# Layer norm and gate of a spatial-gating head group in pairs of 128-token tiles: one Gelu over 1024 columns for two tiles, PSUM emptied by a Copy, and a 2 KB GpSimd descriptor reserve

## The chip, the cores and the metric

The kernel runs on one NeuronCore of a Trainium2 chip. The metric is device time in microseconds (us) of one execution, lower is better. The time before the change is 2483.25 us, the median of three runs that lie between 2481.99 and 2483.38 us.

The core has five engines that run their own instruction streams in order and meet through semaphores: TensorE (PE, with its weight loads shown apart as PEld), VectorE (DVE), ScalarE (ACT), GpSimd (POOL) and SyncE (SP), which issues most DMA transfers. Matmul results land in PSUM banks; the other operands live in SBUF.

## The reference

One layer of an encoder over 2048 positions with 1024 channels. Only the first group of heads ("A", a gated MLP) is touched by the change; the second ("B", attention with a forget gate) runs beside it.

```python
h = rms_norm(x, norm_mix_g)
z = h @ w_in                                   # 1024 -> 2*512 + 3*512 + 8 columns
u_a = gelu(z[..., 0:512], approximate=False)
v_a = gelu(z[..., 512:1024], approximate=False)
# spatial gating, per block of 128 positions and per head of 64 channels
mu  = mean(v, axis=-1); var = mean((v - mu) ** 2, axis=-1)
vn  = (v - mu) * rsqrt(var + EPS) * ln_g
mixed = einsum('hts,bnshd->bnthd', masked w_s, vn) + b_s
out_a = u * mixed
# group B: softmax(q k^T / 8 + c[t] - c[s]) v, causal, c = cumsum(log sigmoid(f))
x = x + concat(out_a, out_b) @ w_out
x = x + conv_ffn(rms_norm(x)); out = rms_norm(x)
```

## The kernel before

All matrix products are in float32 split into a high and a low part, three matmuls for one (`mm3`, lines 202 to 212): line 207 (high by high), line 209 (high by low) and line 211 (low by high). Tokens are worked in two halves of 1024. Phase A of a half makes the projection `z`: keys and queries with channels on the partitions (`channels`, into `kx` and `qx`), values, and the two gated parts with tokens on the partitions (`token_major`). Phase B is attention; it has no stage of its own in the beginning but is fed as filler between the matmuls of phase A.

**The gated stage.** `gated` (line 467) is called at the end of half 0 and at the start of half 1, so the two calls follow each other. Each runs `token_major(512)`, the columns of `v`, and then `token_major(0)`, the columns of `u`: eight tiles of 128 tokens each, 24 matmuls (8 chunks by 3) of 512 columns per tile into one of two PSUM banks of the tag "mm". That makes 4 x 8 x 24 = 768 matmuls of this kind.

- For a tile of `v`, `a_layernorm` (line 520) applies Gelu straight from the PSUM bank into an SBUF tile "ln" (line 525, ACT) and then works by heads: sum (530, DVE), times 1/64 (531), subtract (532), square (535, ACT), sum (538, DVE), times 1/64 plus EPS (539), power of -0.5 (540, POOL), scale (543, DVE), times the gain (544, POOL). The result lies in one half of a pair tile "vn".
- For a tile of `u`, `a_mixed` (line 491) is called before every second tile and already works on pairs: the masked mixing matrix by the pair "vn" (498, PE) and the bias (500, DVE). `a_gate` (line 503) applies Gelu from PSUM (507, ACT), multiplies by "vn" (508, DVE) and, later, transposes the product on PE (`turn`, through line 182), splits it (188 on ACT, 189 on DVE) and stores both parts to DRAM (`mixh`, `mixl`, by SP).

**What sets the order.** `tick` counts the matmuls of `mm3`. `defer(n, fn)` runs `fn` in the program n matmuls later; `behind(n, fn)` does the same and also puts an order edge after the last matmul on the engine that the edge concerns. So the steps of the layer norm are spread at 5, 17, 25 and 40 matmuls after their tile, the gate's multiply at 5 and its transposes at 30 (`GATE_LAG`). The attention filler takes one step every 3.5 (half 0) or 4.0 (half 1) matmuls (`RATES`). A step of the filler is a score tile (lines 713 and 714 on PE, 717 or 719 on DVE for the row minimum, 722 on ACT for Exp with a sum), or a tile of the second pass (774 and 775 on PE, 778 on DVE, Exp at 780 on ACT, the split at 785 on ACT and 786 on DVE, and the product with the values at 762 and 763 on PE). Score tiles use three PSUM banks of the tag "s". From this the framework's planner makes one fixed order per engine, by priorities and by costs of its own.

Gelu and Exp (and Ln) need different function tables on ACT. The compiled program has an `ACT_TABLE_LOAD` wherever the table changes; the profile gives it the line of the instruction that needs it. Copy and Square have none in front of them.

Weights come as 128x1024 units: a DMA into "raw", a cast on POOL (149) and the rest on DVE (161).

The last argument of the program's constructor (line 1456) reserves a part of SBUF per partition for the descriptors of transfers that GpSimd issues. Those are 35 of the whole program, none of them in the gated stage: 22 at line 895, 11 at line 937 and 2 at line 1240.

Of the kernel before, what the change touches and what calls it, by code (L numbers as in the profile page):

```python
# [18 lines left out]
P = 128  # L19
# [6 lines left out]
TB = 512  # L26
# [9 lines left out]
GATE_LAG = 30  # L36
# [1 line left out]

BUFS = {
    "raw": 2, "rawl": 3, "whi": 5, "wlo": 5, "thi": 2, "tlo": 2, "acc": 4,  # L40
# [11 lines left out]
def f32(ap):  # L52
    return ap.bitcast(F32)
# [26 lines left out]
class Block:  # L80
# [323 lines left out]
    def a_half(self, half):  # L404
        nc, sp, pp = self.nc, self.sp, self.ap
# [17 lines left out]
        def token_major(col):  # L423
            us = [self.load_unit(self.w_in[:, 2 * j:2 * j + 2, col:col + 512], 512) for j in range(4)]
            wh = [us[k // 2][0][:, k % 2, :] for k in range(KC)]
            wl = [us[k // 2][1][:, k % 2, :] for k in range(KC)]
            for t in range(8):
                ps = self.til(pp, [P, TB], F32, "mm")
                tsl = slice((t % 4) * P, (t % 4 + 1) * P)
                self.mm3(ps, part(t // 4, 0, tsl), part(t // 4, 1, tsl), wh, wl)  # L430
                yield t, ps
# [35 lines left out]
        def gated():  # L467
            vns = []
            for t, ps in token_major(512):
                if t % 2 == 0:  # L470
                    vns.append(self.til(sp, [P, 2, TB], F32, "vn"))
                self.a_layernorm(ps, vns[-1][:, t % 2, :])
            for t, ps in token_major(0):
                if t % 2 == 0:
                    self.a_mixed(vns[t // 2])
                self.a_gate(half * 2 + t // 4, t % 4, ps, vns[t // 2][:, t % 2, :])
                if half == 0 and t % 4 == 3:
                    self.a_norm(1, t // 4, self.scales[t // 4], 14 if t == 3 else 16, 9 if t == 3 else 6)

        if half == 0:  # L480
            keys_queries()
            values()
            self.start_fill(self.b_stream([(h, tb) for tb in range(4) for h in range(8)]), RATES[0])
            gated()
        else:
            self.rate = RATES[1]
            gated()
            values()
            keys_queries()
# [10 lines left out]
                nc.vector.tensor_tensor(v[:, :, t, :], pg[:, :, t, :],  # L500
                                        self.sgb[:, 4 * q:4 * q + 4].unsqueeze(2).broadcast_to([P, 4, 64]), op=ALU.add)

    def a_gate(self, blk, t, pu, vn):

        nc, sp, pp = self.nc, self.sp, self.ap
        u = self.til(sp, [P, TB], F32, "u")
        nc.scalar.activation(u, pu, AF.Gelu)  # L507
        self.behind(5, lambda: nc.vector.tensor_tensor(u, u, vn, op=ALU.mult))

        def turn():  # L510
            hi = self.til(sp, [P, TB], F32R, "st")
            lo = self.til(sp, [P, TB], F32R, "st")
            self.transpose_split(pp, "tp", [u[:, c * P:(c + 1) * P] for c in range(4)], None, hi, lo)
            for r, dst in ((hi, self.mixh[blk]), (lo, self.mixl[blk])):
                self.dma(dst[0:512, t * P:(t + 1) * P].rearrange("(c p) t -> p c t", p=P),
                         f32(r).rearrange("p (c t) -> p c t", c=4))

        self.defer(GATE_LAG, turn)

    def a_layernorm(self, ps, vn):  # L520
        nc, sp = self.nc, self.sp
        h3 = lambda t: t.rearrange("p (h d) -> p h d", h=8)
        bc = lambda t: t.unsqueeze(2).broadcast_to([P, 8, 64])
        v = self.til(sp, [P, TB], F32, "ln")
        nc.scalar.activation(v, ps, AF.Gelu)  # L525
        mu, s2, r = [self.til(sp, [P, 8], F32, "lns") for _ in range(3)]


        def mean():
            nc.vector.tensor_reduce(mu, h3(v), axis=AX.X, op=ALU.add)  # L530
            nc.vector.tensor_scalar(mu, mu, 1.0 / 64, None, ALU.mult)
            nc.vector.tensor_tensor(h3(v), h3(v), bc(mu), op=ALU.subtract)

        def squares():
            nc.scalar.activation(vn, v, AF.Square)

        def variance():
            nc.vector.tensor_reduce(s2, h3(vn), axis=AX.X, op=ALU.add)
            nc.vector.tensor_scalar(s2, s2, 1.0 / 64, EPS, ALU.mult, ALU.add)
            nc.gpsimd.tensor_tensor(r, s2, self.mhalf, op=ALU.pow)  # L540

        def scale():
            nc.vector.tensor_tensor(h3(v), h3(v), bc(r), op=ALU.mult)
            nc.gpsimd.tensor_tensor(vn, v, self.lng, op=ALU.mult)

        for n, fn in ((5, mean), (17, squares), (25, variance), (40, scale)):
            self.behind(n, fn)

    def a_forget(self, half, b):
# [917 lines left out]
```

## Time and profile before

| What | Value |
|---|---|
| Runs | 2481.99, 2483.38, 2483.25 us; median 2483.25 us |
| Profiled execution | 2483.0 us |
| Its span, first to last instruction | 2481.3 us, so 1.7 us lie around it |
| Granted TensorE clock over the span | 0.995 |
| Busy share of the span | PE 98%, PEld 80%, DVE 70%, ACT 55%, POOL 14% |
| Gated stage (both halves) | about 186 to 466 us from the start of the span |

How to read it: a busy share is a mean over stages with different limits. Durations of matmuls are modelled and overlap, so a busy PE is not PE at its best pace; the distance from one matmul's start to the next shows the pace. "Idle before" is the time an engine stood still ahead of an instruction, and the arrow names what ended it. Line numbers are those of the kernel before.

### The profile page before, as it was taken

What the parts mean: (1) busy time and instruction counts of PE and PEld (TensorE: products, weight loads), DVE (VectorE), ACT (ScalarE), POOL (GpSimd) and SP (SyncE); (2) the same over time, 40 slices, a digit from 0 to 9 for tenths busy, and PEclk for the clock granted to TensorE, in tenths of its full rate; (3) what the DMA queues carried; (4) which work ended last, traced back from release to release, by engine and by line L of the source; (5) the groups of instructions that cost most, each with busy time, mean ns of one, the idle gap of its engine ahead of it and who ended that gap; (6) DMA issues with size and microseconds to landing.
All of it is one profiled execution on the core that took longest, in us unless ns stands there. A gap on an engine that the chain in (4) does not pass through costs nothing.

```text
span 2481.3 us, 33045 instructions
## 1 busy us (share of the span) xinstructions
PE 2430.5 (98%) x11082; PEld 1995.2 (80%) x11082; DVE 1742.9 (70%) x3116; ACT 1367.4 (55%) x2651; POOL 335.6 (14%) x343
## 2 busy tenths in 40 slices
PE   7998999999999999999999999999999999999998
PEld 5786878878788888888888888878888887888887
DVE  6237677655456878878787775488888887957776
ACT  4327778554355556766677673265555555444443
POOL 3214233010014111211111110100000000001000
PEclk9999999999999999999999999999999999999999
DMA  6863544766867545555555455412222228538633
GB/s 205 239 155 89 155 144 127 189 157 186 284 186 244 156 149 169 176 169 163 175 161 159 154 176 202 144 60 86 92 77 77 93 78 310 169 98 286 210 117 122
DMA packets 346246, 396.35 MB, mean 160 GB/s; under 512 B 52924, under 2 KB 222084, under 8 KB 344652
## 3 DMA queue, kind: packets, MB, share of 16 engines
q1 hardware_dynamic: 341036, 370.11, 48.8%
q0 software_dynamic: 5040, 24.12, 2.5%
q8 instruction: 88, 1.44, 0.2%
q14 instruction: 82, 0.67, 0.1%
HBM read 300.56 MB, written 93.72 MB: 159 GB/s over the span
## 4 chain that ended last, share of the span: by engine, by line
PE 81%; DVE 3%; ACT 2%; DMA 2%; issue 1%; POOL 1%; SPq 0%; DVEq 0%; POOLq 0%; ACTq 0%
PE D L1323 16%; PE mm L209 11%; PE mm L207 11%; PE mm L211 11%; PE A L1120 3%; PE A L1122 3%; PE A L1121 3%; PE o L763 2%; PE o L762 2%; PE s L714 2%; PE s L774 2%; PE s L775 2%; PE s L713 2%; PE B L1121 2%; PE B L1122 2%; PE B L1120 2%
## 5 line engine op out<-in xcount | busy, mean ns | idle before, releaser
L207 PE MATMUL mm<-thi,whi 128*128 128x512 f32 x960 | 378.4, 394 | 0.7 <-DVE vn L417 0.7
L209 PE MATMUL mm<-tlo,whi 128*128 128x512 f32 x960 | 377.5, 393 | 0.0
L211 PE MATMUL mm<-thi,wlo 128*128 128x512 f32 x960 | 377.1, 393 | 0.2 <-DVE wlo L161 0.2
L207 PE MATMUL mm<-whi,thi 128*128 128x512 f32 x640 | 254.4, 399 | 1.8 <-ACT ln L525 1.0
L209 PE MATMUL mm<-wlo,thi 128*128 128x512 f32 x640 | 253.5, 396 | 0.3 <-DVE wlo L161 0.2
L149 POOL TENSOR_SCALAR whi<-raw 128x1024 fp32r<-128x1024 f32 x108 | 127.0, 1176 | 935.6 <-PE mm L209 581.5
L211 PE MATMUL mm<-whi,tlo 128*128 128x512 f32 x640 | 253.3, 396 | 0.0
L722 ACT ACTIVATE s<-s,part 128x512 f32<-128x512 f32 (+3 forms) x257 | 150.7, 587 | 116.7 <-DVE part L717 60.3
L207 PEld LDWEIGHTS mm<-thi,whi 128*128 128x128 f32 x960 | 180.9, 188 | 39.1 <-DVE vn L417 1.1
L211 PEld LDWEIGHTS mm<-thi,wlo 128*128 128x128 f32 x960 | 180.9, 188 | 37.9 <-DVE wlo L161 0.7
L209 PEld LDWEIGHTS mm<-tlo,whi 128*128 128x128 f32 x960 | 180.9, 188 | 37.6
L786 DVE TENSOR_TENSOR pl<-e,ph 128x512 fp32r<-128x512 f32 (+2 forms) x212 | 131.7, 629 | 63.4 <-PE o L763 34.6
L161 DVE TENSOR_TENSOR wlo<-raw,whi 128x1024 fp32r<-128x1024 f32 x108 | 138.2, 1280 | 51.2 <-POOL whi L149 49.7
L780 ACT ACTIVATE e<-s 128x512 f32<-128x512 f32 (+2 forms) x227 | 116.5, 528 | 80.3 <-DVE s L778 38.3
L785 ACT ACTIVATE ph<-e 128x512 fp32r<-128x512 f32 (+2 forms) x212 | 117.4, 562 | 47.5 <-PE o L762 36.7
L207 PEld LDWEIGHTS mm<-whi,thi 128*128 128x128 f32 x640 | 121.7, 190 | 26.5 <-ACT u L507 1.6
L1323 PE MATMUL D<-wl,xh 128*128 128x512 f32 x368 | 141.3, 389 | 0.0
L209 PEld LDWEIGHTS mm<-wlo,thi 128*128 128x128 f32 x640 | 121.7, 190 | 24.3 <-DVE wlo L161 1.0
L1323 PE MATMUL D<-wh,xh 128*128 128x512 f32 x368 | 140.8, 389 | 0.2 <-DVE xo L1401 0.2
L211 PEld LDWEIGHTS mm<-whi,tlo 128*128 128x128 f32 x640 | 121.7, 190 | 24.0
L1323 PE MATMUL D<-wh,xl 128*128 128x512 f32 x368 | 137.2, 389 | 0.0
L717 DVE TENSOR_REDUCE part<-s 128x1 f32<-128x512 f32 x144 | 94.9, 683 | 29.0 <-PE s L714 28.9
(1883 smaller groups left out, 5837.6 us busy)
## 6 DMA issues: line engine op xcount, KB each, us to landing
raw<-in_w_up_dram SPq DMA_DIRECT2D x72, 512.0 KB
m<-kx SPq DMA_DIRECT2D x133, 256.0 KB
m<-kx SPq DMA_DIRECT2D x160, 136.0 KB
x<-act SPq DMA_DIRECT2D x84, 256.0 KB
raw<-in_w_in_dram SPq DMA_DIRECT2D x40, 512.0 KB
v<-vd SPq DMA_DIRECT2D x66, 256.0 KB
x<-in_x_dram SPq DMA_DIRECT2D x24, 512.0 KB
raw<-in_w_out_dram SPq DMA_DIRECT2D x24, 512.0 KB
```

What stands on the lines that cost most here:

```text
L149: self.cast_ins = self.nc.gpsimd.tensor_scalar(out, in_, 1.0, 0.0, ALU.mult, ALU.add).ins
L161: nc.vector.tensor_tensor(lo, raw, f32(hi), op=ALU.subtract)
L207: mm(ps, lhsT=ah[k], rhs=bh[k], start=k == 0, stop=False)
L209: mm(ps, lhsT=ah[k], rhs=bl[k], start=False, stop=False)
L211: self.last_mm = mm(ps, lhsT=al[k], rhs=bh[k], start=False, stop=k == n - 1).ins
L722: nc.scalar.activation(ps[:, :n], ps[:, :n], AF.Exp, scale=-1.0, bias=dst, accum_out=ls[:, tt, sb:sb + 1])
L785: nc.scalar.activation(ph[:, c], e[:, c], AF.Copy)
L786: nc.vector.tensor_tensor(pl[:, c], e[:, c], f32(ph[:, c]), op=ALU.subtract)
L1120: mm(ps, lhsT=xh[:, ks], rhs=yh[:, k, :], start=fresh and k == 0, stop=False, **kw)
L1121: mm(ps, lhsT=xh[:, ks], rhs=yl[:, k, :], start=False, stop=False, **kw)
L1122: mm(ps, lhsT=xl[:, ks], rhs=yh[:, k, :], start=False, stop=k == 3, **kw)
L1323: nc.tensor.matmul(bank[t], lhsT=x[i][:, ts], rhs=w[k], start=fresh and j == 0 and i + k == 0, stop=last and i == 1, **kw)
```

## The change

The layer norm and the gate take two tiles of 128 tokens at a time. Each PSUM bank is emptied by a Copy on ACT into one half of a pair tile of 1024 columns ("ln" for `v`, "u" for `u`). After the second tile, one Gelu over 1024 columns runs in place in SBUF, 3 matmuls later, and the following steps work on 1024 columns with 16 heads: sum, subtract, square, power, scale and the gate's multiply. The gain's multiply on POOL stays in two pieces of 512. The steps stand at 3, 9, 20, 28 and 44 matmuls after the pair's last matmul, the gate's multiply at 9 and the two tiles' transposes at 30 and 38. The pair tiles are twice as large; "ln" has 2 buffers for 3, "u" keeps 2, and the reserve for GpSimd's descriptors goes from 8192 to 2048 bytes per partition.

```diff
-    "x": 4, "st": 4, "ln": 3, "vn": 4, "u": 2, "lns": 9, "fs": 9, "fr": 3,
+    "x": 4, "st": 4, "ln": 2, "vn": 4, "u": 2, "lns": 9, "fs": 9, "fr": 3,
@@ gated
             for t, ps in token_major(512):
                 if t % 2 == 0:
+                    v = self.til(sp, [P, 2, TB], F32, "ln")
+                nc.scalar.activation(v[:, t % 2, :], ps, AF.Copy)
+                if t % 2:
                     vns.append(self.til(sp, [P, 2, TB], F32, "vn"))
-                self.a_layernorm(ps, vns[-1][:, t % 2, :])
+                    self.a_layernorm(v, vns[-1])
             for t, ps in token_major(0):
                 if t % 2 == 0:
                     self.a_mixed(vns[t // 2])
-                self.a_gate(half * 2 + t // 4, t % 4, ps, vns[t // 2][:, t % 2, :])
+                    u = self.til(sp, [P, 2, TB], F32, "u")
+                nc.scalar.activation(u[:, t % 2, :], ps, AF.Copy)
+                if t % 2:
+                    self.a_gate(half * 2 + t // 4, t % 4, u, vns[t // 2])
@@ a_gate
-        u = self.til(sp, [P, TB], F32, "u")
-        nc.scalar.activation(u, pu, AF.Gelu)
-        self.behind(5, lambda: nc.vector.tensor_tensor(u, u, vn, op=ALU.mult))
+        self.behind(3, lambda: nc.scalar.activation(u, u, AF.Gelu))
+        self.behind(9, lambda: nc.vector.tensor_tensor(u, u, vn, op=ALU.mult))
...
-        self.defer(GATE_LAG, turn)
+        self.defer(GATE_LAG, lambda: turn(0))
+        self.defer(GATE_LAG + 8, lambda: turn(1))
@@ a_layernorm
-        v = self.til(sp, [P, TB], F32, "ln")
-        nc.scalar.activation(v, ps, AF.Gelu)
-        mu, s2, r = [self.til(sp, [P, 8], F32, "lns") for _ in range(3)]
+        mu, s2, r = [self.til(sp, [P, 16], F32, "lns") for _ in range(3)]
+        half16 = self.mhalf[:, 0:1].broadcast_to([P, 16])
+        def gelu():
+            nc.scalar.activation(v, v, AF.Gelu)
...
-            nc.gpsimd.tensor_tensor(r, s2, self.mhalf, op=ALU.pow)
+            nc.gpsimd.tensor_tensor(r, s2, half16, op=ALU.pow)
 
         def scale():
             nc.vector.tensor_tensor(h3(v), h3(v), bc(r), op=ALU.mult)
-            nc.gpsimd.tensor_tensor(vn, v, self.lng, op=ALU.mult)
+            for j in range(2):
+                nc.gpsimd.tensor_tensor(vn[:, j, :], v[:, j, :], self.lng, op=ALU.mult)
 
-        for n, fn in ((5, mean), (17, squares), (25, variance), (40, scale)):
+        for n, fn in ((3, gelu), (9, mean), (20, squares), (28, variance), (44, scale)):
             self.behind(n, fn)
@@ kernel
-    nc = _bacc.Bacc("TRN2", target_bir_lowering=False, num_devices=1, dynamic_dma_scratch_size=8192)
+    nc = _bacc.Bacc("TRN2", target_bir_lowering=False, num_devices=1, dynamic_dma_scratch_size=2048)
```

More of the change, by code (lines that the diff above doesn't have):

```diff
@@ L501, in a_mixed, with a_gate, turn, a_layernorm @@
                                         self.sgb[:, 4 * q:4 * q + 4].unsqueeze(2).broadcast_to([P, 4, 64]), op=ALU.add)
-    def a_gate(self, blk, t, pu, vn):
+    def a_gate(self, blk, t, u, vn):
         nc, sp, pp = self.nc, self.sp, self.ap
-        u = self.til(sp, [P, TB], F32, "u")
-        nc.scalar.activation(u, pu, AF.Gelu)
-        self.behind(5, lambda: nc.vector.tensor_tensor(u, u, vn, op=ALU.mult))
-        def turn():
+        self.behind(3, lambda: nc.scalar.activation(u, u, AF.Gelu))
+        self.behind(9, lambda: nc.vector.tensor_tensor(u, u, vn, op=ALU.mult))
+        def turn(j):
             hi = self.til(sp, [P, TB], F32R, "st")
             lo = self.til(sp, [P, TB], F32R, "st")
-            self.transpose_split(pp, "tp", [u[:, c * P:(c + 1) * P] for c in range(4)], None, hi, lo)
+            self.transpose_split(pp, "tp", [u[:, j, c * P:(c + 1) * P] for c in range(4)], None, hi, lo)
+            tj = t - 1 + j
             for r, dst in ((hi, self.mixh[blk]), (lo, self.mixl[blk])):
-                self.dma(dst[0:512, t * P:(t + 1) * P].rearrange("(c p) t -> p c t", p=P),
+                self.dma(dst[0:512, tj * P:(tj + 1) * P].rearrange("(c p) t -> p c t", p=P),
                          f32(r).rearrange("p (c t) -> p c t", c=4))
-        self.defer(GATE_LAG, turn)
-    def a_layernorm(self, ps, vn):
+        self.defer(GATE_LAG, lambda: turn(0))
+        self.defer(GATE_LAG + 8, lambda: turn(1))
+    def a_layernorm(self, v, vn):
         nc, sp = self.nc, self.sp
-        h3 = lambda t: t.rearrange("p (h d) -> p h d", h=8)
-        bc = lambda t: t.unsqueeze(2).broadcast_to([P, 8, 64])
-        v = self.til(sp, [P, TB], F32, "ln")
-        nc.scalar.activation(v, ps, AF.Gelu)
-        mu, s2, r = [self.til(sp, [P, 8], F32, "lns") for _ in range(3)]
+        h3 = lambda t: t.rearrange("p t (h d) -> p (t h) d", h=8)
+        bc = lambda t: t.unsqueeze(2).broadcast_to([P, 16, 64])
+        mu, s2, r = [self.til(sp, [P, 16], F32, "lns") for _ in range(3)]
+        half16 = self.mhalf[:, 0:1].broadcast_to([P, 16])
+        def gelu():
+            nc.scalar.activation(v, v, AF.Gelu)
         def mean():
```

## The prediction

> **What bounds the kernel now.** I read the page first, then the busy times by stretch, the waits of PE, the instruction groups of ACT inside the gated stage, and last the timeline round one wait. The page says that PE sets the time:
>
> ```profile
> span 2481.3 us, 33045 instructions
> PE 2430.5 (98%) x11082; PEld 1995.2 (80%) x11082; DVE 1742.9 (70%) x3116; ACT 1367.4 (55%) x2651; POOL 335.6 (14%) x343
> ```
>
> The change leaves PE's matmuls as they are, so it can only win back time in which PE stands still or runs slowly. Busy times by stretch (length, then PE, PEld, DVE, ACT, POOL, granted clock, DMA share, GB/s), for the gated stage and for the stage behind it:
>
> ```profile
> 186.00:466.00 280.00, 267.04 (x1329) 219.39 (x1328) 199.73 (x446) 208.53 (x366) 82.07 (x65) 0.98 0.46 134
> 466.00:600.00 134.00, 134.00 (x628) 106.77 (x627) 75.05 (x173) 68.26 (x153) 9.78 (x8) 1.00 0.66 176
> ```
>
> PE idles 280.00 - 267.04 = 13.0 us in the gated stage and nothing in the 134 us behind it, where the same filler runs without Gelu. ACT is at 208.53 / 280 = 74% in the first and 51% in the second. The waits of PE in the gated stage (total us, times, longest):
>
> ```profile
> PE s L774 <- ACT s L722: 7.3, 6, 2.3
> PE o L762 <- ACT ph L785: 1.4, 2, 1.0
> PE s L774 <- ACT e L780: 1.3, 2, 1.0
> PE mm L207 <- ACT ln L525: 1.0, 1, 1.0
> PE mm L207 <- ACT u L507: 0.9, 2, 0.6
> ```
>
> These five add to 11.9 us of the 13.0, and all wait for ACT; the remaining rows name DVE, none a DMA. The groups of ACT in the stage (busy us, mean ns | idle before):
>
> ```profile
> L722 ACT ACT_TABLE_LOAD x17 | 21.8, 1283 | 5.4 <-DVE part L719 3.1 <-DVE part L717 2.0
> L507 ACT ACT_TABLE_LOAD x16 | 20.5, 1283 | 0.3
> L525 ACT ACT_TABLE_LOAD x15 | 19.2, 1283 | 0.3
> L780 ACT ACT_TABLE_LOAD x13 | 16.7, 1283 | 0.2
> L535 ACT ACTIVATE vn<-ln 128x512 f32<-128x512 f32 x16 | 10.1, 633 | 20.7 <-DVE ln L532 13.5 <-issue 7.2
> L507 ACT ACTIVATE u<-mm 128x512 f32<-128x512 f32 x16 | 9.6, 599 | 0.2
> L525 ACT ACTIVATE ln<-mm 128x512 f32<-128x512 f32 x16 | 9.5, 599 | 0.2
> L188 ACT ACTIVATE st<-tp 128x512 fp32r<-128x512 f32 x15 | 8.9, 594 | 0.7 <-PE tp L182 0.7
> ```
>
> Nearly every Gelu pays a table load (15 + 16 for 32), and the filler's next Exp pays one back (17 + 13): 61 loads, 78.2 us. How that becomes a PE wait, in the timeline (start, us, engine, line; idle before and its releaser in brackets), ACT, DVE and PE in turn, and then three stretches of 20 us with ACT's busy time and the granted clock:
>
> ```profile
> 347.66 1.28 ACT L525 ACT_TABLE_LOAD   x1
> 348.95 0.60 ACT L525 ACTIVATE ln<-mm 128x512 f32<-128x512 f32 x1
> 351.07 1.28 ACT L722 ACT_TABLE_LOAD   x1 [1.53 <-DVE part L719]
> ```
>
> ```profile
> 349.58 0.69 DVE L530 TENSOR_REDUCE lns<-ln 128x8 f32<-128x512 f32 x1 [1.07 <-ACT ln L525]
> 350.30 0.17 DVE L531 TENSOR_SCALAR lns<-lns 128x8 f32<-128x8 f32 x1
> 350.38 0.56 DVE L719 CUSTOM_DVE_ANT_0 s<-s,mask 128x384 f32<-128x384 f32 x1
> ```
>
> ```profile
> 350.62 0.39 PE L209 MATMUL mm<-wlo,thi 128*128 128x512 f32 x1
> 350.85 0.39 PE L211 MATMUL mm<-whi,tlo 128*128 128x512 f32 x1
> 353.10 0.47 PE L774 MATMUL s<-t,m 128*128 128x384 f32 x1 [1.86 <-ACT s L722]
> 353.38 0.51 PE L775 MATMUL s<-t,m 128*128 128x384 f32 x1
> 353.68 0.63 PE L207 MATMUL mm<-whi,thi 128*128 128x512 f32 x1
> ...
> 356.67 0.45 PE L209 MATMUL mm<-wlo,thi 128*128 128x512 f32 x1
> ```
>
> ```profile
> 206.00:226.00 20.00, 12.83 (x22) 0.91 0.18 59
> 246.00:266.00 20.00, 13.60 (x23) 0.91 0.49 144
> 346.00:366.00 20.00, 16.86 (x32) 0.91 0.30 85
> ```
>
> Gelu comes late because of its load, the layer norm's sum on DVE waits for it, the filler's row minimum (719) is queued behind that sum, ACT loads the Exp table only then, and PE, out of score banks, waits 1.86 us. After that the clock is down: the seven matmuls from 353.68 to 356.67 take 2.99 us instead of 7 x 0.23 = 1.61, so 1.4 us more. Three stretches show such a drop, 4.2 us together. **What is at stake is 11.9 + 4.2 = 16.1 us.**
>
> [...]
>
> **The change part by part.** *ACT.* Rows for operations of 1024 columns, and what they replace on DVE:
>
> ```profile
> L1237 ACT ACTIVATE cv<-ts 128x1024 f32<-128x1024 f32 x22 | 23.3, 1060 | 16.0 <-DVE ts L1233 16.0
> L1239 DVE TENSOR_TENSOR ts<-ts 128x1024 f32<-128x1024 f32 x22 | 26.8, 1220 | 0.0
> L530 DVE TENSOR_REDUCE lns<-ln 128x8 f32<-128x512 f32 x16 | 10.9, 684 | 14.7 <-ACT ln L525 14.6
> ```
>
> Removed: 78.2 of loads, 9.6 + 9.5 of Gelu, 10.1 of squares, 107.4 us. Added: 32 Copies out of PSUM at 0.594 (L188, which never has a load ahead) are 19.0; 16 Gelus at 1.06 are 17.0; 8 squares at 1.06 are 8.5; 16 loads for Gelu and at most 16 back are 32 x 1.283 = 41.1. That is 85.6 us, so ACT does 21.8 us less and falls from 74% to 67% of the stage.
>
> [...]
>
> *Banks.* The two rows of L207 that wait for Gelu (1.0 + 0.9) go: a Copy frees the bank after 0.6 us with no load ahead. What covers the Copy is the second "mm" bank, filled in 24 matmuls; without that cover it would cost 32 x 0.6 = 19 us.
>
> *Visits of Gelu.* The other ACT waits and the clock, 10.0 + 4.2 = 14.2 us, hang on ACT changing tables: 31 visits become 16, so half of it, 7.1 us, goes. Each visit that is left holds ACT 1.06 - 0.60 = 0.46 us longer and DVE 1.22 - 0.68 = 0.54 us longer at a piece, up to 1.0 us together. This price is not in the trace. Below, it is nothing: most visits cause no wait today. Above, every one of the 16 pays 1.0, 16 us. Only three waits today come with the clock drop, that is, are at the limit; half of that with some margin is one visit, so I take 1.0 us.
>
> *DVE.* Two operations of 512 (2 x 0.684) become one of 1.22, 0.15 less; with five such per pair and 8 pairs, 40 x 0.15 = 6 us less work. I count it at nothing, since DVE is 71% busy and its order matters more than its sum.
>
> *POOL and the reserve.*
>
> ```profile
> L540 POOL TENSOR_TENSOR lns<-lns,mhalf 128x8 f32<-128x8 f32 x16 | 27.8, 1736 | 66.1 <-DVE lns L539 56.7 <-DVE m L730 4.8 <-DVE mx L728 3.2
> L544 POOL TENSOR_TENSOR vn<-ln,lng 128x512 f32<-128x512 f32 x16 | 24.1, 1507 | 19.8 <-DVE ln L543 11.0 <-ACT ph L195 3.2 <-DVE lns L531 3.2
> L176 POOL TENSOR_TENSOR rstd<-rs,mhalf 128x1 f32<-128x1 f32 x16 | 9.5, 593 | 1.3
> act<-va POOLq DMA_DIRECT2D x22, 512.0 KB, 4.5
> ```
>
> The power of 16 columns lies between 1.74 and 2 x 1.74 = 3.47 us; on the line through 1 and 8 columns, 0.593 and 1.736, it is 1.736 + 8 x 0.163 = 3.04. Behind it on DVE waits the scale step, and behind that the filler. A matmul's slot in the stage is 280 / 768 = 0.365 us, so the scale stands 16 x 0.365 = 5.8 us after the variance, which needs 1.22 + 0.17 (L531's like) + 3.04 = 4.4: covered with 1.4 us to spare, where there were 15 x 0.365 - (0.68 + 0.17 + 1.74) = 2.9 before. If that cover were gone, 8 pairs at up to 1.4 us each would lose 11 us. The pair tile "ln" must be free 72 matmuls after its last one; scale (44), 1.22 and two products of 1.51 leave over 5 us. The stores of two tiles come 8 matmuls apart rather than 24; SP's filler loads behind them are covered, since no PE wait of the stage names a DMA. The smaller reserve costs nothing unless a transfer must wait for the one before: 4.5 us to land against a spacing of a whole pair of up-projection units, with POOL 14% busy. If that cover were gone, each of the 35 would hold POOL for about 4 us.
>
> **Sum.** 1.9 + 7.1 - 1.0 = 8.0 us out of the profiled execution's 2483.0 (1.7 more than its span): **2475.0 us**. The median of the runs, 2483.25, is the same to 0.01%. Behind the stage nothing takes the gain back that I can see: PE has no idle time from 466 to 600 us.
>
> **The rivals.**
>
> 1. *The waits only move* (no change by measure). For it: the 1.86 us wait hung on the order DVE has, sum before row minimum, and that order stays with a longer sum; the mean stands 6 matmuls, 2.2 us, behind a Gelu that needs 1.28 + 1.06 = 2.34. Against it: half as many such places. Then only the 1.9 us of the banks are sure: about 2481.
> 2. *The longer hold breaks the filler* (slower). Place: the three score banks at L774. A visit now keeps Exp off ACT for 1.28 + 1.06 + 1.28 = 3.6 us, before 3.2. If that is past what three banks cover, each visit makes a wait like the longest, 2.3 us, with 1.4 of slow clock: 3.7. Today's stake is met from 16.1 / 3.7 = 4.4 visits on; with 6 to 8 of 16 it is 22 to 30 us against 16.1, so 2489 to 2497. For it: waits of 2.3 already exist at 3.2. Against it: most of 31 visits cause none.
> 3. *It clears the stage.* All idle time and slow clock go, 13.0 + 4.2: 2483.0 - 17.2 = 2466. For it: the stage behind, with ACT at 51%, has none. Against it: ACT stays at 67%.
> 4. *Loads do not fall to 32*, since the planner may put Exp between the Copies and the Gelu without a saving: not likely, as Copy needs no table and the Gelus are 16 in number.
>
> **How the numbers follow.** About 0.2%, 5 us, is what a measurement of this kernel can tell from no change. Forecast (gain of 5 to 12 us) 0.43; rival 3 0.12; rival 1 0.25; rival 2 0.19; rival 4 0.01, at no change. So faster 0.55, same 0.26, slower 0.19. The likeliest one's own range is 2471 to 2478. The range to hold 8 in 10 takes the stake and a little for a new order of the planner's below, 2464, and rival 2's first half above, 2491.
>
> **What would show it.** In the stage: about 32 table loads with Gelu's rows 16; no PE wait at L207 for ACT; ACT near 187 us; PE's idle time near 6 us and one or two stretches below full clock instead of three. Wrong would be: PE idle at 13 us or more with half the loads; a wait at the Copy for "ln"; the scale step waiting for POOL in every pair; or a difference that lies behind 466 us.

## The result and the profile after

The changed kernel takes 2470.30 us (median of 5 runs, 2464.07 to 2473.17); the kernel before took 2481.99 us in the same series (5 runs, 2480.32 to 2483.38). The ratio is 0.995, with a 95% interval from 0.9935 to 0.9965. The profiled execution took 2470.3 us against 2483.0. So the change is faster by 11.7 us, 0.5%; the forecast was 8.0 us faster, 2475.0, in a range of 2464 to 2491.

Line numbers after the change are higher than before: 713 is now 724, 717 is 728, 719 is 730, 722 is 733, 762 is 773, 763 is 774, 774 is 785, 780 is 791, 785 is 796 and 786 is 797. The two Copies are 472 and 480, the two Gelus 537 and 512, the power 550, the scale 553 and the gain 555.

The head of the page after, and the busy times by stretch (columns as in the prediction):

```profile
span 2468.5 us, 32938 instructions
PE 2423.2 (98%) x11082; PEld 1992.3 (81%) x11082; DVE 1738.5 (70%) x3060; ACT 1341.4 (54%) x2629; POOL 329.2 (13%) x335
```

```profile
0.00:186.00 186.00, 171.00 (x793) 135.79 (x794) 76.80 (x152) 63.68 (x118) 44.81 (x69) 1.00 0.72 205
186.00:466.00 280.00, 273.00 (x1390) 228.68 (x1389) 203.31 (x405) 191.97 (x358) 77.48 (x56) 0.99 0.49 143
466.00:600.00 134.00, 134.00 (x627) 107.25 (x626) 73.57 (x166) 64.66 (x147) 9.06 (x8) 1.00 0.65 174
```

PE does the same 11082 matmuls. In the gated stage its idle time is 280.00 - 273.00 = 7.0 us, before 13.0, and ACT is busy for 191.97 us, before 208.53. PE ran 1390 matmuls in the same 280 us, before 1329: the stage itself became shorter. The waits of PE in it (total us, times, longest):

```profile
PE o L774 <- DVE pl L797: 2.1, 2, 1.7
PE s L758 <- DVE m L742: 1.9, 1, 1.9
PE s L724 <- DMA t<-qx: 1.9, 1, 1.9
PE s L785 <- ACT s L733: 0.5, 1, 0.5
```

The first row of before, 7.3 us for Exp (then L774 for L722), is down to 0.5 us, and nothing waits at L207 for Gelu any more. What is left waits for DVE and for one transfer. The groups of ACT in the stage, the table loads and the new operations (busy us, mean ns | idle before):

```profile
L733 ACT ACT_TABLE_LOAD x10 | 12.8, 1283 | 0.2
L537 ACT ACT_TABLE_LOAD x8 | 10.3, 1283 | 0.1
L512 ACT ACT_TABLE_LOAD x8 | 10.3, 1283 | 0.1
L480 ACT ACTIVATE u<-mm 128x512 f32<-128x512 f32 x16 | 9.6, 599 | 8.3 <-PE mm L211 8.2
L472 ACT ACTIVATE ln<-mm 128x512 f32<-128x512 f32 x15 | 8.7, 595 | 3.5 <-PE mm L211 3.4
...
L512 ACT ACTIVATE u<-u 128x1024 f32<-128x1024 f32 x8 | 8.5, 1061 | 0.1
L537 ACT ACTIVATE ln<-ln 128x1024 f32<-128x1024 f32 x8 | 8.5, 1060 | 0.1
L791 ACT ACT_TABLE_LOAD x5 | 6.4, 1283 | 0.1
```

Loads: 10 + 8 + 8 + 5 = 31 in place of 61, 39.8 us in place of 78.2. Each kernel has one load more in this window, for a small Exp of the filler (L748, before L737), so all in all there are 32 for 62. Both Gelu rows have 8 instructions and 8 loads, one load per visit.

**Where the time came from.** The windows above do not hold the same work in the two kernels, so I also counted along the work itself. Between the starts of two matmuls of the projection, I subtracted from the time that passed the length of every matmul in between at full pace (0.227 us for 512 columns, 0.175 for 384, 0.119 for 256, 0.108 for 128, read off the timelines). What is left is time that PE lost to waits and to a slow clock. The full-pace work is 2391.4 us in both kernels; the loss went from 73.5 to 60.7 us:

| Part (by projection matmuls) | lost before, us | lost after, us | difference |
|---|---|---|---|
| ahead of the gated stage (first 24 tiles) | 16.8 | 12.5 | -4.3 |
| gated stage (tiles 24 to 56) | 27.1 | 13.8 | -13.3 |
| behind it | 29.6 | 34.4 | +4.8 |

Two of the three rows are not what the prediction was about. The first row turned out to have a cause of its own. The last is worth little: counted in the same way, `before_no_gelu` (below), which has the order of the kernel before, loses 33.7 us there and not 29.6, and over the 14 profiles of this case that row lies between 27.8 and 36.2.

### The profile page after: what moved, and what is told of

The parts are those of the page before. It is cut to its first block, busy times and chain, and to the rows that moved or that the text cites. A ratio compares the mean times of both kernels' runs of the same rounds, so it can differ in the third digit from the quotient of the medians.

```text
span 2468.5 us, 32938 instructions
## 1 busy us (share of the span) xinstructions
PE 2423.2 (98%) x11082; PEld 1992.3 (81%) x11082; DVE 1738.5 (70%) x3060; ACT 1341.4 (54%) x2629; POOL 329.2 (13%) x335
## 4 chain that ended last, share of the span: by engine, by line
PE 83%; DMA 6%; DVE 5%; issue 2%; ACT 2%; POOL 1%; SPq 0%; POOLq 0%; DVEq 0%; ACTq 0%
PE D L1334 14%; PE mm L211 12%; PE mm L207 12%; PE mm L209 12%; PE A L1131 3%; PE A L1133 3%; PE A L1132 3%; PE o L774 2%; PE o L773 2%; PE s L786 2%; PE s L785 2%; PE B L1133 2%; PE B L1132 2%; PE B L1131 2%; PE s L724 2%
## 5 line engine op out<-in xcount | busy, mean ns | idle before, releaser
L207 PE MATMUL mm<-thi,whi 128*128 128x512 f32 x960 | 377.8, 394 | 1.7 <-DVE vn L417 1.4
L207 PE MATMUL mm<-whi,thi 128*128 128x512 f32 x640 | 253.7, 397 | 3.2 <-DVE acc L860 3.1
L207 PEld LDWEIGHTS mm<-thi,whi 128*128 128x128 f32 x960 | 180.5, 188 | 40.6 <-DVE vn L417 2.0
L797 DVE TENSOR_TENSOR pl<-e,ph 128x512 fp32r<-128x512 f32 (+2 forms) x212 | 136.6, 651 | 74.0 <-PE o L774 41.0
L207 PEld LDWEIGHTS mm<-whi,thi 128*128 128x128 f32 x640 | 121.0, 189 | 27.5 <-DVE acc L860 3.5
L209 PEld LDWEIGHTS mm<-wlo,thi 128*128 128x128 f32 x640 | 121.0, 189 | 23.3 <-DVE wlo L161 0.4
```

The lines of the kernel that those rows point to most:

```text
L207: mm(ps, lhsT=ah[k], rhs=bh[k], start=k == 0, stop=False)
L209: mm(ps, lhsT=ah[k], rhs=bl[k], start=False, stop=False)
L797: nc.vector.tensor_tensor(pl[:, c], e[:, c], f32(ph[:, c]), op=ALU.subtract)
```

## The experiments

Nearly every edit of this kernel makes the planner lay out all engines' order anew. That mattered for reading the runs: two kernels with different orders can differ by several us for reasons that have nothing to do with the edit. `reserve_only` and the two kernels without Gelu kept PE's and DVE's order to the instruction, and `late_steps` changed 42 of PE's 11082 places. Ratios are against the kernel before in the same series, with 95% intervals. The last three columns are PE's lost time of the one profile of each kernel, counted as above, good to about 0.2 us; the kernel before has 16.8, 27.1 and 29.6.

| Kernel | median us | ratio | lost ahead | in the stage | behind |
|---|---|---|---|---|---|
| reserve_only | 2484.68 | 1.0003 [0.9994, 1.0013] | 17.0 | 28.8 | 30.9 |
| late_steps | 2483.54 | 1.0004 [0.9995, 1.0014] | 16.0 | 27.7 | 32.0 |
| copy_only | 2482.99 | 1.0 [0.9991, 1.001] | 19.1 | 27.0 | 27.8 |
| gate_pairs_only | 2482.93 | 1.0003 [0.9993, 1.0014] | 17.1 | 23.3 | 35.3 |
| early_ring | 2478.35 | 0.9987 [0.9978, 0.9996] | 12.9 | 26.1 | 29.9 |
| copy_early_ring | 2487.21 | 1.0017 [1.0008, 1.0027] | 12.1 | 25.8 | 36.2 |
| gelu_each | 2475.84 | 0.9969 [0.9959, 0.9979] | 12.2 | 17.8 | 32.2 |
| norm_pairs_only | 2475.22 | 0.9964 [0.9951, 0.9977] | 11.8 | 20.7 | 33.3 |
| the changed kernel | 2470.30 | 0.995 [0.9935, 0.9965] | 12.5 | 13.8 | 34.4 |
| gain_on_dve | 2468.99 | 0.9942 [0.9927, 0.9957] | 12.9 | 11.2 | 34.3 |
| before_no_gelu | 2466.41 | 0.9929 [0.9912, 0.9945] | 13.9 | 9.4 | 33.7 |
| dve_by_512 | 2464.34 | 0.9926 [0.9911, 0.9941] | 13.9 | 10.4 | 32.1 |
| after_no_gelu | 2461.58 | 0.9914 [0.9899, 0.9929] | 13.1 | 6.1 | 32.4 |

The stage column is the steadiest: the six kernels that work single tiles with Gelu, under several orders, lose 25.8 to 28.8 us there. It is one profile per kernel all the same; `reserve_only`, with the order of the kernel before, differs from it by 1.7 us.

### The small reserve alone

```diff
-    dynamic_dma_scratch_size=8192
+    dynamic_dma_scratch_size=2048
```

> The kernel before with the reserve for GpSimd's descriptors at 2048 bytes for 8192, nothing else. Theory A (the gain comes from the halved visits of Gelu to ACT): no change, 2477 to 2486 us, and the 35 transfers of GpSimd land in 4 to 6 us as before. Rival (part of the gain or of what was lost behind the stage comes from the reserve, since 4.4 us of the profiled gain lie ahead of the gated stage): a difference of 3 us or more, ahead of or behind the stage.

Measured: 2484.68 us (10 runs, 2480.43 to 2486.91) against 2483.41 (25 runs). The planned order of PE and DVE is that of the kernel before. The reserve costs nothing that can be measured and brings nothing. The transfers land in 4.7 to 5.2 us, before in 4.5 to 5.2 (medians of the three groups).

### The change with one Gelu per tile

```diff
                 nc.scalar.activation(v[:, t % 2, :], ps, AF.Copy)
+                self.behind(3, lambda x=v[:, t % 2, :]: nc.scalar.activation(x, x, AF.Gelu))
...
-        for n, fn in ((3, gelu), (9, mean), (20, squares), (28, variance), (44, scale)):
+        for n, fn in ((9, mean), (20, squares), (28, variance), (44, scale)):
```

and the same for `u`. All else stays in pairs, so the 32 visits of Gelu are back.

> The changed kernel, but Gelu runs on each tile of 128 tokens by itself, in place, 3 matmuls after that tile's Copy: the pairs on DVE and POOL and the Copies stay, the table visits are back at 32. Theory A (visits of Gelu): most of the gain is lost, 2478 to 2490 us, with some 60 table loads in the stage and PE waiting for ACT again. Rival B (fewer, wider DVE operations and the bank freed by a Copy make the gain): 2468 to 2474 us.

Measured: 2475.84 us (9 runs, 2469.89 to 2480.13), halfway between the kernels, so neither range was met. The table loads of the stage by group:

```profile
L734 ACT ACT_TABLE_LOAD x16 | 20.5, 1283 | 0.3
L482 ACT ACT_TABLE_LOAD x15 | 19.2, 1283 | 0.3
L473 ACT ACT_TABLE_LOAD x12 | 15.4, 1283 | 0.2
L792 ACT ACT_TABLE_LOAD x11 | 14.1, 1283 | 0.2
```

So there are 54 loads for 31 in these groups; in the whole profile it is 65, before 71, after 41, and 9 with no Gelu. The 24 more cost 2475.84 - 2470.30 = 5.5 us against the changed kernel, and 17.8 - 13.8 = 4.0 us in the stage. The other half of the gain does not hang on the number of visits.

### One half of the change at a time

`norm_pairs_only` pairs the layer norm and leaves the gate as before; `gate_pairs_only` pairs the gate and leaves the layer norm.

```diff
@@ gated, in norm_pairs_only
-                nc.scalar.activation(u[:, t % 2, :], ps, AF.Copy)
-                if t % 2:
-                    self.a_gate(half * 2 + t // 4, t % 4, u, vns[t // 2])
+                self.a_gate(half * 2 + t // 4, t % 4, ps, vns[t // 2][:, t % 2, :])
```

> Layer norm in pairs as in the changed kernel, gate by single tiles as before. Theory A: 8 visits of Gelu fewer for the layer norm, about half of the gain: 2473 to 2479 us, and the waits fall in the layer norm's part of each half. Rival B (the order on DVE: sum before the filler's row minimum, which only the layer norm has): nearly all of the gain, 2468 to 2473.

> Gate in pairs as in the changed kernel, layer norm by single tiles as before. Theory A: the other half of the gain, 2473 to 2479 us. Rival B (the layer norm's order on DVE): hardly any gain, 2478 to 2484.

Measured: 2475.22 us (5 runs, 2468.98 to 2476.19) for the layer norm, 2482.93 us (10 runs, 2479.63 to 2491.46) for the gate. The first lies in theory A's range, the second in rival B's. Each has 18 table loads fewer than the kernel before (53 in the whole profile), as theory A wants, and yet one brings about 8 us and the other nothing by itself. In the stage it looks more even: 6.4 us less is lost with the layer norm in pairs and 3.8 with the gate. What hides the second in the time lies behind the stage (35.3 for 29.6), a row that moves by several us from profile to profile. In `norm_pairs_only` the wait that a Copy removes for the gate is still there and is the largest PE wait of the stage:

```profile
PE mm L207 <- ACT u L510: 4.1, 3, 1.5
```

The two halves also differ in something away from the gated stage. Of the waits of PE from 0 to 186 us, the second row of the kernel before and of `gate_pairs_only`, and the first two of the changed kernel:

```profile
PE s L713 <- DMA t<-qx: 2.7, 1, 2.7
```

```profile
PE s L717 <- DMA t<-qx: 3.7, 1, 3.7
```

```profile
PE mm L182 <- DVE rstd L361: 7.5, 1, 7.5
PE tp L182 <- DVE tlo L192: 2.3, 2, 1.4
```

The first score matmul of the filler waits for the queries' transfer in the first two kernels and not in the third. The layer norm's half has the tag "ln" at 2 buffers, the gate's half keeps it at 3. But "ln" is also the tag of four tiles of other sizes that the program makes long before (squares of the RMS norm, a mask, and two of the forget gate), so their order hangs on the same number.

### The early users of "ln" on a ring of their own

```diff
-    "ln": 3,
+    "ln": 3, "le": 2,
...
-            junk = self.til(sp, [P, D], BF16, "ln")
+            junk = self.til(sp, [P, D], BF16, "le")
```

and the same for the other three early tiles, in the kernel before (with the small reserve).

> The kernel before with the users of the tag "ln" that come ahead of the gated stage (squares of the first rows, the triangle, the forget gate's rows) on a ring of their own with two buffers of 2 KB, as many as the changed kernel has; the layer norm keeps its three; the reserve at 2048 bytes pays for it. In the planned order the filler's first score matmul on PE then stands where the changed kernel has it, at place 462 and not 386. Theory D (part of the gain is the planner's order ahead of the stage, a PE wait of 2.7 us for a transfer of queries and the slow clock behind it): 2476 to 2481 us, no wait of PE for a transfer near 98 us, and the first 16 blocks of 24 matmuls 4 to 5 us shorter. Theory B alone (all of the gain is the layer norm's work in the stage): 2482 to 2486 us.

Measured: 2478.35 us (10 runs, 2476.21 to 2480.84) against 2481.46 (25 runs): 3.1 us faster, by the interval 1.0 to 5.5. The wait for the queries is gone from the first 186 us:

```profile
PE mm L182 <- DVE rstd L361: 7.4, 1, 7.4
PE tp L182 <- DVE tlo L192: 2.0, 2, 1.5
PE mm L207 <- DVE vn L417: 2.0, 1, 2.0
```

In the profile 466 matmuls start ahead of the filler's first score matmul, as in the changed kernel; in the kernel before it is 394. The first 16 blocks are done at 126.1 us for 130.7, the 4 to 5 us that theory D expects. The wait was found in each of the 6 profiles of this case in which the early tiles run on three buffers and in none of the 8 in which they run on two. What it costs is more than the wait, as the timeline of before shows (start, us; idle before in brackets):

```profile
97.54 0.39 PE L211 MATMUL mm<-thi,wlo 128*128 128x512 f32 x1
100.63 0.68 PE L713 MATMUL s<-m,t 96*128 96x128 f32 x2 [2.70 <-DMA t<-qx]
101.10 0.63 PE L207 MATMUL mm<-thi,whi 128*128 128x512 f32 x1
...
103.67 0.63 PE L207 MATMUL mm<-thi,whi 128*128 128x512 f32 x1
```

Seven matmuls start 0.43 us apart from 101.10 on, where 0.23 is the full pace: 1.4 us more. So about 3 us can be had by one digit in the table of buffers, 85 us ahead of the gated stage, without pairs. That the changed kernel gains them in the same way is likely, since its wait is gone too and its loss ahead of the stage fell by 4.3 us.

### The Copies and the later steps without pairs

`late_steps` only moves the steps to 9, 20, 28 and 44 and the gate's multiply to 9. `copy_only` does that and empties the bank by a Copy, with Gelu in place 3 matmuls later, on single tiles. `copy_early_ring` is `copy_only` with the early ring and the small reserve.

```diff
-        nc.scalar.activation(v, ps, AF.Gelu)
+        nc.scalar.activation(v, ps, AF.Copy)
...
-        for n, fn in ((5, mean), (17, squares), (25, variance), (40, scale)):
+        for n, fn in ((3, lambda: nc.scalar.activation(v, v, AF.Gelu)), (9, mean), (20, squares), (28, variance), (44, scale)):
```

> The kernel before with only the places of the steps moved to the changed kernel's: sum at 9 for 5 matmuls, squares at 20, variance at 28, scale at 44, the gate's multiply at 9. Theory B3 (DVE waits for Gelu because the sum is queued too early, and the filler's row minimum behind it): DVE's waits for Gelu, 25.1 us before, fall below 12, and 2474 to 2480 us. If the order is not it: 2480 to 2485.

> The kernel before with a Copy out of PSUM and Gelu in place 3 matmuls later, for each tile of 128 tokens by itself, and the layer norm's and the gate's steps at the changed kernel's places (9, 20, 28, 44; 9); no pairs, no fewer table loads, 32 Copies more. Theory B1 (what helps is that the bank is freed and Gelu is taken out of the way of the filler's order): most of the gain inside the stage, 2472 to 2478 us. Theory B2 (what helps is DVE's and POOL's work in pairs): no gain, 2480 to 2487. Theory A (table visits): slower than before, since ACT does 19 us more, 2484 to 2495.

> Copies, Gelu in place and the late places of the steps, all by single tiles, with the early users of "ln" on their own ring of two: it is the run with Gelu on each tile (2475.8 us) less the pairs on DVE and POOL and in the squares, with the same plan ahead of the stage. Theory B2 (the pairs of the steps, that is half as many places in the filler's order, are worth most of what that run gained): 2478 to 2484 us. If the Copies and the plan ahead make it: 2473 to 2477.

Measured: 2483.54 us (10 runs, 2479.11 to 2484.96), 2482.99 us (10 runs, 2481.0 to 2485.03) and 2487.21 us (10 runs, 2482.88 to 2492.15). None of the three gains anything. Moving the steps does not even shorten DVE's waits for Gelu, 25.2 us in `late_steps` and 25.1 before. Theory A is not borne out either: `copy_only` has 32 Copies more and is no slower.

`copy_early_ring` is 8.9 us slower than `early_ring` (7.4 by the ratios), where `copy_only` is at no change from the kernel before. The stage gives the same answer on both bases: 25.8 for 26.1 us lost, and 27.0 for 27.1. So Copies and later steps without pairs are worth nothing in the stage, and the difference lies behind it (36.2 for 29.9).

`copy_early_ring` and `gelu_each` both have Gelu on each tile, the same Copies and early tiles on two buffers; the first works single tiles and the second pairs, and the second is 11 us faster, 8.0 us of it in the stage. That speaks for the paired steps themselves, although `copy_early_ring` lies above both ranges. Why they help is not shown: it is not DVE's shorter work, since `dve_by_512` (below) gives that back and loses less still; half as many places at which steps cut into the filler's order would fit, but no run varies that alone.

### Without Gelu, order kept

To price the table loads with nothing else moving, both kernels were run with Copy in place of Gelu (this leaves Gelu out of the result):

```diff
-        nc.scalar.activation(v, ps, AF.Gelu)
+        nc.scalar.activation(v, ps, AF.Copy)
```

and likewise at each other Gelu of this group. The instructions of every engine and their order are as in the kernel each was made from; only the loads are gone.

> The kernel before with Gelu left out: a Copy stands in its place, so the output is not the reference's, and the compiled program has no table loads for Gelu and none back. PE's and DVE's planned order is the same as before, instruction for instruction. Theory A (the visits of Gelu are what is lost in the stage): the stage's lost time of PE falls from 27 us to under 8, 2458 to 2466 us. Theory B (the order of the layer norm's steps in between the filler's is the larger part): 2468 to 2476.

> The changed kernel with Gelu left out in the same way (a Copy of 1024 columns in its place, the output is not the reference's). Theory A: what the loads still cost is half of what they cost before, 2462 to 2466 us. Theory B: the loads that are left are hidden, within 3 us of the changed kernel's 2470.

Measured: 2466.41 us (4 runs, 2462.76 to 2467.14) and 2461.58 us (4 runs, 2460.94 to 2462.58). The gated stage of the first, then of the second:

```profile
186.00:466.00 280.00, 276.17 (x1415) 231.56 (x1414) 211.93 (x462) 138.51 (x323) 80.92 (x64) 1.00 0.52 149
```

```profile
186.00:466.00 280.00, 279.18 (x1429) 234.30 (x1428) 205.86 (x411) 152.22 (x330) 78.00 (x56) 1.00 0.52 149
```

In the kernel before, all loads together are worth 2482.55 - 2466.41 = 16.1 us (17.6 by the ratio, 13.7 to 21.8 by its interval). That the stake of the prediction is 16.1 too is right in size, and luck to the tenth. In the changed kernel they are worth 2470.30 - 2461.58 = 8.7 us, of two series whose kernels before lie 0.6 us apart. So what the change gains through the loads is 16.1 - 8.7 = 7.4 us (8.7 if the ratios are used, 0.0071 - 0.0036 of 2482), and 2466.41 - 2461.58 = 4.8 us (3.7 by the ratios) are gained with no load in either kernel. The runs of one kernel spread over 2 to 9 us, so each of these differences is good to a few us. The first time lies 0.4 us above the range of its theory A, the second 0.4 us below the range of its own; the stage's loss falls to 9.4 us in the first, where theory A said under 8.

A single load comes out nearly alike in three ways: 16.1 us for 62 loads is 0.26 us, 8.7 for 32 is 0.27, and the 5.5 of `gelu_each` for 24 is 0.23. That is the best evidence that half of the loads is half of their cost. In the stage's lost time the three are 17.7, 7.7 and 4.0 us, which is less even (0.29, 0.24 and 0.17 a load): there the pairs seem to make a load cheaper as well.

Of the gain with no load, the two profiles have 3.3 us in the stage, 0.8 ahead of it and 1.3 behind it. So the 3 us of `early_ring` can't simply be taken off the 4.8: `before_no_gelu` still has the wait for the queries (2.0 us), and yet only 0.8 us more is lost ahead of the stage.

### The long pieces on DVE

The prediction charged 1.0 us for the longer pieces. Two timelines of the changed kernel show what such a piece can do: DVE around 230 us, and GpSimd in the same time.

```profile
227.23 2.06 DVE L161 TENSOR_TENSOR wlo<-raw,whi 128x1024 fp32r<-128x1024 f32 x1
229.22 0.29 DVE L789 TENSOR_TENSOR s<-s,maskT 128x128 f32<-128x128 f32 x1
229.41 2.11 DVE L161 TENSOR_TENSOR wlo<-raw,whi 128x1024 fp32r<-128x1024 f32 x1
231.44 1.35 DVE L797 TENSOR_TENSOR pl<-e,ph 128x128 fp32r<-128x128 f32 x1
```

```profile
225.19 3.03 POOL L149 TENSOR_SCALAR whi<-raw 128x1024 fp32r<-128x1024 f32 x2
228.19 4.46 POOL L555 TENSOR_TENSOR vn<-ln,lng 128x512 f32<-128x512 f32 x2
```

While GpSimd ends a cast and multiplies by the gain, DVE's weight split takes 2.06 and 2.11 us instead of its median of 1.22, and GpSimd's two products 2.23 us each instead of a median of 1.30. The next piece on DVE (L797), which the product on PE waits for, comes late: that is the 1.7 us in the first row of PE's waits after. Two kernels were made from the changed one. `dve_by_512` cuts DVE's five steps of a pair into two pieces of 512, with Gelu, squares and power still on pairs. `gain_on_dve` also moves the gain's product to DVE.

```diff
-            nc.vector.tensor_reduce(mu, h3(v), axis=AX.X, op=ALU.add)
+            for j in range(2):
+                nc.vector.tensor_reduce(m8(mu, j), h8(v, j), axis=AX.X, op=ALU.add)
...
@@ gain_on_dve, beside that
-                nc.gpsimd.tensor_tensor(vn[:, j, :], v[:, j, :], self.lng, op=ALU.mult)
+                nc.vector.tensor_tensor(vn[:, j, :], v[:, j, :], self.lng, op=ALU.mult)
```

> The changed kernel with every wide operation of DVE in the layer norm and the gate cut in two of 512 columns again; Gelu, squares and power stay in pairs. Theory B2 (fewer, wider operations of DVE): part of the gain is lost, 2473 to 2480 us. Rival 2's mechanism (a piece of 1.22 us holds up the filler's row minimum): faster than the changed kernel, 2463 to 2468. If neither counts: within 3 us of the changed kernel's 2470.

> The changed kernel with DVE's steps in pieces of 512 (2464.3 us) and, on top, the multiply by the gain on DVE instead of GpSimd: 16 operations of 512 more on DVE, 11 us, and 25 us less on GpSimd. Theory E (DVE and GpSimd hold each other up: operations of 1.22 us that took 2.06 beside GpSimd's multiply): DVE's 128x1024 and 128x512 operations are at their short times everywhere and it is 2459 to 2464 us. If DVE's added work counts more: 2465 to 2472.

Measured: 2464.34 us (4 runs, 2461.21 to 2465.74), the fastest kernel of this case that computes everything, and 2468.99 us (4 runs, 2465.85 to 2471.01). The row of the weight split in the changed kernel and then in `gain_on_dve`:

```profile
L161 DVE TENSOR_TENSOR wlo<-raw,whi x16: 1206/1225/2326, 227.2 to 449.8; 128x1024 fp32r<-128x1024 f32 x16
```

```profile
L161 DVE TENSOR_TENSOR wlo<-raw,whi x16: 1209/1220/1225, 226.0 to 443.9; 128x1024 fp32r<-128x1024 f32 x16
```

With the gain on DVE the lengthened splits are gone (shortest, median and longest are now alike), though three of the layer norm's pieces of 512 still take 1.5 us for 0.69. Yet the kernel is no faster than `dve_by_512`, whose longest split still takes 2.285 us. So the long splits of the changed kernel's stage go with GpSimd's products, but they are not what decides. Cutting DVE's pieces brings 6 us against the changed kernel by the medians and by the ratios, whose intervals overlap slightly; in the stage 10.4 us is lost for 13.8. At the same time 1903 of PE's 11082 places changed. Whether the shorter hold of DVE or the new order does it could not be told apart. Theory B2, that fewer and wider operations of DVE are worth something, is not borne out: cutting them costs nothing. `gain_on_dve` lies in the range in which DVE's added work counts more.

## Why the prediction was right, and where it was off

**The stake.** Right. 16.1 us was read from PE's waits for ACT (11.9) and three clock drops (4.2); with all loads gone and the order kept, the kernel before is 16.1 us faster (13.7 to 21.8). The stake was a count of waits in one profile, so its size follows from the trace, and the equal tenth is luck. It is also not a cleared stage, though rival 3's 2466 is met by `before_no_gelu` at 2466.41: 3.8 us of PE's idle time is left in the window, and 9.4 us of lost time in the stage.

**Loads and ACT.** Right. 32 loads forecast, 32 measured (the 61 counted before left out the one at L737); ACT near 187 us forecast, 191.97 measured. The window of 280 us now holds more of the filler, since the stage is shorter. No wait at L207 for ACT is left. In the stage neither Copy nor Square has a load ahead of it; in the whole profile of before the only one at a Square (L358, at 0.79 us) is the first load of the program.

**Half of the visits, half of the cost; the longer visit at 1.0.** Right within what the runs can tell: 1.9 + 7.1 - 1.0 = 8.0 us forecast for all that hangs on the loads, 7.4 measured between the kernels with and without Gelu. The halved visits alone, less their longer hold, were put at 6.1; from `gelu_each` to the changed kernel it is 5.5. The 7.1 and the 1.0 were not measured apart. `norm_pairs_only`, whose largest PE wait is still the gate's bank, supports the first term.

**Power.** The power of 16 columns was put at 3.04 us; the row of GpSimd in the stage after says 3.038:

```profile
L550 POOL TENSOR_TENSOR lns<-lns,mhalf 128x16 f32<-128x16 f32 x8 | 24.3, 3038 | 68.5 <-DVE lns L549 68.5
```

**The scale's cover** was wrong. It was put at 1.4 us to spare, and DVE waits for the power 6 times in 8 pairs, at most 1.6 us:

```profile
DVE ln L553 <- POOL lns L550: 5.8, 6, 1.6
```

The cover was not there before the change either: the same wait was 4.7 us in all, 5 times, where the prediction read 2.9 us to spare. The sum took each operation at its usual length and DVE free in between. In one place of the changed kernel the power takes 3.73 us, and the wait goes on to PE, here in DVE's and then PE's timeline:

```profile
369.64 2.07 DVE L553 TENSOR_TENSOR ln<-ln,lns 128x1024 f32<-128x1024 f32 x1 [1.38 <-POOL lns L550]
371.64 1.01 DVE L741 TENSOR_SCALAR m<-mx 128x4 fp32r<-128x4 f32 x1
372.56 0.15 DVE L747 TENSOR_TENSOR lw<-mx,part 128x8 f32<-128x8 f32 x1
372.63 2.33 DVE L161 TENSOR_TENSOR wlo<-raw,whi 128x1024 fp32r<-128x1024 f32 x1
374.88 1.22 DVE L742 SCALAR_TENSOR_TENSOR m<-mx,m 128x4 fp32r<-128x4 f32 x1
```

```profile
376.16 0.27 PE L758 MATMUL s<-ident,m 128*8 128x128 f32 x1 [1.93 <-DVE m L742]
```

DVE is busy without a break from the scale to the piece that PE waits for. So the second row of PE's waits after begins with the power on GpSimd and is made longer by a scale and a split of over 2 us; what each of the two adds was not measured. The reserve cost nothing that could be measured (2484.68 us against 2483.41), as forecast; the 4 us for which a transfer would hold GpSimd were an estimate and were not shown.

**PE's idle time and the clock.** Near 6 us idle was forecast, 7.0 measured. One or two clock drops for three were forecast, and one is left: after the wait of 1.9 us for the queries at 344.80, seen in the two 20 us stretches that it straddles (ACT's busy time, granted clock):

```profile
326.00:346.00 20.00, 14.84 (x30) 0.97 0.41 114
346.00:366.00 20.00, 12.54 (x24) 0.94 0.20 63
```

**What the sum lacked.** The gain was 11.7 us and not 8.0. Two places of the prediction fall short.

- It says that the change can only win back time in which PE stands still or runs slowly, and then looks for that time in the gated stage and behind it, not ahead of it. It took the order of the other stages as given; a new order of the planner's had a place in its range, but not in its sum. With "ln" at 2 buffers the filler starts later in PE's order, and a wait of 2.7 us and its slow clock vanish 85 us ahead of the stage. By `early_ring` that is 3.1 us (1.0 to 5.5).
- It put the steps in pairs at nothing, as 6 us less of DVE's work whose order matters more. With Gelu on each tile in both, the pairs save 8.0 us in the stage (25.8 to 17.8); with no Gelu in either kernel it is 3.3. Its reason, that DVE's sum of work does not count, holds: `dve_by_512` has that work back and is faster. What in the pairs helps stays open.

These two and the 7.4 us can't be added up, since the pairs also seem to change what a load costs. The loss of 4.8 us behind the stage, which the prediction named as a sign of being wrong, lies within what that row does by itself: with the order of the kernel before, three profiles have 29.6, 30.9 and 33.7 there.

**DVE's longer pieces.** The prediction charged 1.0 us for the longer visits. That PE's waits left in the stage are mostly for DVE, and that pieces of 512 run 6 us faster, speaks for a higher price of the long pieces; because of the new order this is an argument and not a proof.

**The rivals.** That waits only move: some did, to DVE and to a transfer, but 6.0 us of idle time went. That the longer hold breaks the filler: PE's waits for the score banks fell from 7.3 + 1.3 to 0.5 us at a visit of 3.6 us, so in this profile three banks cover it. That the stage clears: not with 32 loads; it takes `after_no_gelu`, where PE is idle for 0.8 of 280 us.

## What to carry to other kernels

To price a cause that touches only one engine, replace it by something of the same shape that lacks only the cost (here Copy for Gelu) and see that the other engines' order is unchanged: that gave 16.1 and 8.7 us, and the same price of a load in both kernels. Where an edit does move the order, count the lost time stage by stage: six kernels that lie up to 9 us apart in time lose 25.8 to 28.8 us in the gated stage, and most of the scatter lies elsewhere. Where a planner lays out the whole program, look for everything that shares a changed tag or buffer count; the effect can land in a stage that the diff never mentions. And a wait on PE can cost more than its length: in the kernel before, those of 1.86 us at 353.10 and of 2.70 us at 100.63 each had 1.4 us of slow clock behind them.

## What the runs showed of the hardware

**The clock drop is not fixed by the wait's length.** `reserve_only` has the same instructions in the same order as the kernel before. Its wait of 1.86 us for Exp is the one that the prediction followed at 353.10 us, but here no drop comes behind it:

```profile
354.95 0.44 PE L774 MATMUL s<-t,m 128*128 128x384 f32 x1 [1.86 <-ACT s L722]
355.23 0.33 PE L775 MATMUL s<-t,m 128*128 128x384 f32 x1
355.39 0.40 PE L207 MATMUL mm<-whi,thi 128*128 128x512 f32 x1
355.63 0.39 PE L209 MATMUL mm<-wlo,thi 128*128 128x512 f32 x1
```

The next matmuls start 0.23 us apart, where the kernel before showed 0.43; the granted clock is 1.00 from 354 to 359 us, where the kernel before had 0.66 from 352 to 357. In `early_ring` a wait of 1.47 us (at 247.34) is followed by a drop; in the changed kernel one of 1.90 (at 344.80) is and one of 1.93 (at 376.16) is not. So the same wait of 1.86 us was followed by a drop in one execution and not in the other: three drops in one profile are a draw, not a constant.

**DVE and GpSimd took longer side by side, not always both.** The rows at 225 to 232 us above: on DVE 1.22 us becomes 2.06 to 2.11, and on GpSimd 1.30 becomes 2.23. At another place of the changed kernel only GpSimd's operation is longer, a cast that takes 1.76 us right after one of 1.05, while the split beside it stays at 1.23:

```profile
300.16 1.05 POOL L149 TENSOR_SCALAR whi<-raw 128x1024 fp32r<-128x1024 f32 x1 [0.90 <-DMA raw<-in_w_in_dram]
301.63 1.76 POOL L149 TENSOR_SCALAR whi<-raw 128x1024 fp32r<-128x1024 f32 x1 [0.42 <-DMA raw<-in_w_in_dram]
```

```profile
301.24 1.23 DVE L161 TENSOR_TENSOR wlo<-raw,whi 128x1024 fp32r<-128x1024 f32 x1 [0.59 <-POOL whi L149]
```

With the gain's product moved off GpSimd the longest weight split of the stage falls from 2.326 us (2.285 in `dve_by_512`) to 1.225; at 2468.99 us against 2464.34 the run also shows that this did not make the kernel faster. What in the two operations decides which is longer was not shown.

**A table load is mostly hidden.** In the stage of the kernel before, 62 loads of 1.283 us hold ACT for 79.5 us, and taking all of them away is worth 16.1 us, a fifth. A load held ACT for little more than its own length: in the prediction's timeline Gelu starts 1.29 us after its load of 1.28 us does (348.95 and 347.66).
